# A residual block whose feed-forward part is moved behind all mixing and split into an up and a down stage, with seven half products in place of eight

## The chip, the core and the metric

The kernel runs on one core of a Trainium2 chip. A core has a matrix engine (PE, with a separate queue PEld for loading stationary operands), a vector engine (DVE), a scalar engine (ACT), a general engine (POOL), an on-chip memory SBUF of 128 partitions, and an accumulator memory PSUM that PE writes. All transfers between DRAM and SBUF are issued here by one queue, that of the engine SP, in order; 16 DMA engines carry them out. The engines run side by side and wait for one another through semaphores; each executes its own instructions in the order in which they were built. The metric is the time of one execution in microseconds (us).

## The reference

The input x has 2048 tokens of 1024 features, in float32. One layer is computed:

```
h   = RMSNorm_pre(x)
P   = h @ w_in            (columns for attention, RWKV-7 mixing and gates)
yA  = chunk-band attention;   yB = RWKV-7 time mixing (a recurrence over time)
m   = sigmoid(gA) * (yA @ proj_a) + sigmoid(gB) * (yB @ proj_b)
x   = x + RMSNorm_post(m @ w_out)
x   = x + RMSNorm_post2(relu(RMSNorm_pre2(x) @ w_up)^2 @ w_down)
```

The change concerns the last line, the feed-forward part (FFN). Its `w_up` is 1024 x 4096 and its `w_down` 4096 x 1024. The recurrence carries a state from token to token, so the groups of tokens below are mixed in order.

## The kernel before

**Groups and phases.** The tokens are cut into NG = 4 groups of G = 512. `run` (L1114) goes through the groups: `phase_rwkv`, then `phase_attention`, then for groups 0 and 2 `phase_merge` (the gated merge and `w_out`), whose result `o` is stored to the DRAM tiles `od` (L1137); for groups 1 and 3 it calls `phase_ffn` on the pair (0, 1) or (2, 3), which begins with that group's own merge. So the order is: mix 0, mix 1, FFN of both, mix 2, mix 3, FFN of both. `phase_merge` takes a generator and advances it between its own products; for groups 0 and 2 that is `phase_norm`, which loads and normalises x of the next group.

**Precision by three products.** A float32 operand is split (`split`, L68) into a rounded high part, cast by ACT (L69), and the rest, a subtraction by DVE (L70). `mm3` (L72) makes each product of a 128 x 128 stationary block and a 128 x 512 moving block with three matmuls: high by high, high by low, low by high. All of them have one line, L78.

**The FFN.** `residual` (L962) adds x and the normalised `o` of a tile of 128 tokens (L970 to L973), stores it to `x1`, normalises it again (`norm_tile`, L278) and transposes it on PE into the high and low tiles `hh`/`hl` (or `hbh`/`hbl` for the other group). The hidden units are cut into 32 blocks `fb` of 128. `load` brings a 512 KB block of `w_up` and one of `w_down` to SBUF and splits them (L1028 to L1038). `up` (inside `phase_ffn`) multiplies the block with one group's tokens (24 matmuls into `ps_u`), applies relu on ACT (L1045) and the square on DVE (L1046), and splits the result. `down` accumulates two blocks (6 matmuls into a `ps_dn`) and DVE adds them to the sums `u` and `o` in SBUF (L1064). The first two pairs of blocks run for one group alone, and are loaded again for the other, while the residuals of the second group are still being made. `final` normalises the sums (L1074 to L1082) and stores the output (L1083). While the last pair of the first FFN runs, `phase_norm` of group 2 is advanced.

**What sets the order.** Tiles come from pools with a fixed number of buffers; a tile's new use waits until the readers of the old one are done. Weight blocks are loaded into the tag `raw` with two buffers. The instructions are placed by a scheduler when the program is built, so their order on an engine can differ from that of the source; after that it is fixed.

Of the kernel before, what the change touches and what calls it, by code (L numbers as in the profile page):

```python
# [8 lines left out]
F32 = mybir.dt.float32  # L9
# [40 lines left out]
class Block:  # L50
# [70 lines left out]
    def constants(self, ctx):  # L121
# [128 lines left out]
        self.od = [dp.tile([P, D], F32, name=f"od{t}") for t in range(GT)]  # L250
# [711 lines left out]
    def residual(self, mp, pt, g, t, o, gp, g2, hf):  # L962

        nc = self.nc
        ts = slice(t * P, (t + 1) * P)
        x = mp.tile([P, D], F32, tag="x", name="xr")
        nc.sync.dma_start(x, self.a["x"][g * G + t * P : g * G + (t + 1) * P])
        sq = mp.tile([P, D], F32, tag="xn", name="sqo")
        ssq = mp.tile([P, 1], F32, tag="ssqo", bufs=4, name="ssqo")
        nc.scalar.activation(sq, o, AF.Square, accum_out=ssq)  # L970
        r = self.rstd(mp, ssq, 0.25 / D, RMS_EPS, post=0.5)
        nc.vector.scalar_tensor_tensor(o, o, r, gp, op0=ALU.mult, op1=ALU.mult)
        nc.vector.tensor_tensor(x, x, o, ALU.add)  # L973
        nc.sync.dma_start(self.x1[g][ts], x)
        self.norm_tile(mp, pt, x, g2, *hf, ts)


    def phase_ffn(self, gs, following):

        tc, nc, a = self.tc, self.nc, self.a  # L980
        TH = len(gs)
        GB, NT = 2, TH * GT
        with ExitStack() as ctx:
            e = ctx.enter_context
            hb = e(tc.tile_pool(name="hb", bufs=1, reuse_waits="tile"))
            h = [self.alloc_h()] + [
                (hb.tile([P, KB, G], F32R, tag="hh", name="hbh"), hb.tile([P, KB, G], F32R, tag="hl", name="hbl"))
                for _ in gs[1:]
            ]
            hh, hl = zip(*h)  # L990
# [3 lines left out]
            cp = e(tc.tile_pool(name="ffu", bufs=1, reuse_waits="tile"))  # L994
            o = [cp.tile([P, D], F32, name=f"o{t}") for t in range(GT)]
            gains = []

            def before():
                gains.append(self.gain(op, a["post_mix_g"], "g_post", 2))
                gains.append(self.gain(op, a["pre_ffn_g"], "g_pre2", 2))  # L1000
                if TH > 1:
                    with tc.tile_pool(name="prev", bufs=2, side="right", reuse_waits="tile") as qp:
                        for t in range(GT):
                            q = qp.tile([P, D], F32, tag="o", name="o_prev")
                            nc.sync.dma_start(q, self.od[t])
                            self.residual(op, pt, gs[0], t, q, *gains, h[0])
                            yield

            self.phase_merge(gs[-1], o, before())

            def residuals():
                for t in range(GT):
                    self.residual(op, pt, gs[-1], t, o[t], *gains, h[-1])
                    yield

            res = residuals()
            if TH == 1:
                advance(res)
            cp = e(tc.tile_pool(name="ffc", bufs=1, reuse_waits="tile"))
            u = [cp.tile([P, D], F32, name=f"u{t}") for t in range(NT - GT)] + o  # L1020
            fp = e(tc.tile_pool(name="ff", bufs=2, reuse_waits="tile"))
            pn = e(tc.tile_pool(name="ffpd", bufs=4, space=PSUM, reuse_waits="tile"))
            first = [(fg, (th,)) for th in range(TH) for fg in range(2)]
            for fg, ths in first + [(fg, range(TH)) for fg in range(2, FF // P // GB)]:
                fbs = range(fg * GB, (fg + 1) * GB)
                wu, wd, acts = {}, {}, {}

                def load(fb):  # L1028
                    wu[fb] = self.wsplit(
                        a["w_up"][:, fb * P : (fb + 1) * P].rearrange("(k p) n -> p k n", p=P), "w", KB, P  # L1030
                    )
                    raw = self.wp.tile([P, KB, P], F32, tag="raw", name="wdraw")
                    raw = raw.rearrange("p k n -> p (k n)")
                    nc.sync.dma_start(raw, a["w_down"][fb * P : (fb + 1) * P])
                    dh = fp.tile([P, D], F32R, tag="dh", bufs=3, name="dh")
                    dl = fp.tile([P, D], F32R, tag="dl", bufs=3, name="dl")
                    self.split(dh, dl, raw)
                    wd[fb] = dh, dl  # L1038

                def up(fb, th):  # L1040
                    wh, wl = wu[fb]
                    ps = self.pd.tile([P, 512], F32, tag="d", name="ps_u")
                    self.mm3(ps, [(wh[:, k], wl[:, k], hh[th][:, k], hl[th][:, k]) for k in range(KB)])
                    r = fp.tile([P, 512], F32, tag="r", name="r")
                    nc.scalar.activation(r, ps, AF.Relu)  # L1045
                    nc.vector.tensor_tensor(r, r, r, ALU.mult)  # L1046
                    ah = fp.tile([P, 512], F32R, tag="ah", bufs=5, name="ah")
                    al = fp.tile([P, 512], F32R, tag="al", bufs=5, name="al")
                    self.split(ah, al, r)
                    acts[fb, th] = ah, al  # L1050

                def down(th):
                    for t in range(th * GT, (th + 1) * GT):
                        for n in range(2):
                            ps = pn.tile([P, 512], F32, tag="dn", name="ps_dn")
                            ns, sl = slice(n * 512, (n + 1) * 512), slice((t % GT) * P, (t % GT + 1) * P)
                            self.mm3(ps, [
                                (acts[fb, th][0][:, sl], acts[fb, th][1][:, sl], wd[fb][0][:, ns], wd[fb][1][:, ns])
                                for fb in fbs
                            ])  # L1060
                            if fg == 0:
                                nc.vector.tensor_copy(u[t][:, ns], ps)
                            else:
                                nc.vector.tensor_tensor(u[t][:, ns], u[t][:, ns], ps, ALU.add)  # L1064

                def final(th):
                    for t in range(th * GT, (th + 1) * GT):
                        g, ts = gs[th], slice((t % GT) * P, (t % GT + 1) * P)
                        x = op.tile([P, D], F32, tag=("x", "xn")[t % 2], name="x1r")
                        nc.sync.dma_start(x, self.x1[g][ts])  # L1070
                        ssq = op.tile([P, 2], F32, tag="ssq", bufs=4, name="ssqu")
                        for n in range(2):
                            sq = fp.tile([P, 512], F32, tag="r", name="squ")
                            nc.scalar.activation(  # L1074
                                sq, u[t][:, n * 512 : (n + 1) * 512], AF.Square, accum_out=ssq[:, n : n + 1]
                            )
                        nc.gpsimd.tensor_tensor(ssq[:, 0:1], ssq[:, 0:1], ssq[:, 1:2], ALU.add)
                        r = self.rstd(op, ssq[:, 0:1], 1.0 / D, RMS_EPS)
                        nc.vector.tensor_tensor(u[t], u[t], gt, ALU.mult)  # L1079
                        for n in range(2):  # L1080
                            ns = slice(n * 512, (n + 1) * 512)
                            nc.vector.scalar_tensor_tensor(u[t][:, ns], u[t][:, ns], r, x[:, ns], op0=ALU.mult, op1=ALU.add)  # L1082
                        nc.sync.dma_start(self.out[g * G + ts.start : g * G + ts.stop], u[t])  # L1083

                last = fg == FF // P // GB - 1
                if last:
                    gt = self.gain(op, a["post_ffn_g"], "g_post2", 2)
                if last:
                    for fb in fbs:
                        load(fb)  # L1090
                    for th in ths:
                        for fb in fbs:
                            up(fb, th)
                        if th == 0:
                            norm = iter(()) if following is None else self.phase_norm(following, op, pt)
                            advance(norm, 2)
                        if th == TH - 1:
                            advance(norm)
                        down(th)
                        final(th)  # L1100
# [77 lines left out]
```

## Time and profile before

| | us |
|---|---|
| median of three runs | 3515.34 (3513.74 to 3517.0) |
| profiled execution, its own time | 3517.12 |
| span of that execution, first to last instruction | 3515.4 |
| PE busy | 3381.9 |
| DVE busy | 2160.0 |
| ACT busy | 1362.0 |
| POOL busy | 295.7 |

The profile shows one execution. Busy time of PE counts each matmul from its start to a modelled end; matmuls overlap, so that their number in a stretch says more of PE's rate than their durations do. A row of the grouped view gives source line, engine, operation, the tile written and the tiles read, shape and count, then the busy time and the mean of one in ns, then how long the engine sat idle just before and who ended that. A row of the view by stretches gives for each engine busy time and count, then the granted clock of PE, the share of the DMA engines and what they moved in GB/s.

### The profile page before, as it was taken

The page shows a single profiled execution, that of the slowest core. Times are in us where ns is not written, and L with a number is a line of the kernel's source. Part 1 is how long each engine was busy: PE and PEld are TensorE (multiplying, and loading weights), DVE is VectorE, ACT ScalarE, POOL GpSimd, SP SyncE. Part 2 cuts the span into 40 slices and gives each one's busy share as a digit, 9 for nine tenths or more (in the row PEclk, how much of TensorE's full clock was granted, in tenths as well). Part 3 has the DMA queues.
Part 4 walks back from the last instruction along what each step waited for, and adds up shares of the span by engine and source line. Part 5 has one row for each costly group of instructions (what it writes and reads, how often), then busy time and mean ns, then how long its engine had stood idle before and what let it go on. Part 6 is the DMA issues. An engine that isn't in the chain of part 4 may idle for free. (4 is left out here: it accounts for less than half of the span.)

```text
span 3515.4 us, 49861 instructions
## 1 busy us (share of the span) xinstructions
PE 3381.9 (96%) x19617; PEld 2738.6 (78%) x19617; DVE 2160.0 (61%) x3842; ACT 1362.0 (39%) x2355; POOL 295.7 (8%) x572
## 2 busy tenths in 40 slices
PE   7999999999999999999999999999999899999998
PEld 5777777777777888888877778777777778888887
DVE  5775757757767444444667568577577664444446
ACT  4434644436544111122334366444375532122122
POOL 2210002100011000000121000021000100000001
PEclk9999999999999999999999999999999999999999
DMA  4223453225464111111332253531344641111112
GB/s 145 80 85 124 148 185 101 61 91 177 144 220 156 49 50 52 49 48 48 113 100 62 93 178 126 186 98 56 99 152 127 216 144 48 48 48 49 52 50 78
DMA packets 370851, 363.63 MB, mean 103 GB/s; under 512 B 14572, under 2 KB 293296, under 8 KB 370616
## 3 DMA queue, kind: packets, MB, share of 16 engines
q1 hardware_dynamic: 370616, 360.44, 32.4%
q8 instruction: 154, 2.52, 0.3%
q14 instruction: 81, 0.66, 0.1%
HBM read 293.25 MB, written 70.28 MB: 103 GB/s over the span
## 5 line engine op out<-in xcount | busy, mean ns | idle before, releaser
L70 DVE TENSOR_TENSOR wlo<-wraw,whi 128x1024 fp32r<-128x1024 f32 (+1 forms) x368 | 380.9, 1035 | 416.4 <-ACT whi L69 352.0
L69 ACT CAST whi<-wraw 128x1024 fp32r<-128x1024 f32 (+1 forms) x368 | 331.8, 902 | 752.7 <-PE psd L78 400.5
L78 PE MATMUL psd<-hh,whi 128*128 128x512 f32 x1344 | 544.5, 405 | 11.8 <-ACT whi L69 6.6
L78 PE MATMUL psd<-hl,whi 128*128 128x512 f32 x1344 | 542.2, 403 | 0.0
L78 PE MATMUL psd<-hh,wlo 128*128 128x512 f32 x1344 | 539.0, 401 | 0.6 <-DVE wlo L70 0.5
L78 PE MATMUL ps_dn<-dh,ah 128*128 128x512 f32 x1024 | 400.5, 391 | 9.0 <-ACT ah L69 8.9
L78 PE MATMUL ps_dn<-dl,ah 128*128 128x512 f32 x1024 | 398.6, 389 | 0.0
L78 PE MATMUL ps_dn<-dh,al 128*128 128x512 f32 x1024 | 398.2, 390 | 0.0
L69 ACT CAST dh<-wdraw 128x1024 fp32r<-128x1024 f32 x72 | 75.8, 1052 | 625.7 <-PE ps_dn L78 500.5
L78 PEld LDWEIGHTS psd<-hh,whi 128*128 128x128 f32 x1344 | 257.2, 191 | 65.7 <-ACT whi L69 7.4
L78 PEld LDWEIGHTS psd<-hh,wlo 128*128 128x128 f32 x1344 | 257.3, 191 | 51.1 <-DVE wlo L70 2.0
L78 PEld LDWEIGHTS psd<-hl,whi 128*128 128x128 f32 x1344 | 257.7, 192 | 48.6
L1064 DVE TENSOR_TENSOR o<-o,ps_dn 128x512 f32<-128x512 f32 x240 | 164.1, 688 | 147.2 <-PE ps_dn L78 147.1
L78 PEld LDWEIGHTS ps_dn<-dh,ah 128*128 128x128 f32 x1024 | 192.2, 188 | 53.1 <-ACT ah L69 13.7
L78 PEld LDWEIGHTS ps_dn<-dh,al 128*128 128x128 f32 x1024 | 192.2, 188 | 41.0 <-DVE al L70 1.2
L78 PEld LDWEIGHTS ps_dn<-dl,ah 128*128 128x128 f32 x1024 | 192.4, 188 | 39.3
L1064 DVE TENSOR_TENSOR u<-u,ps_dn 128x512 f32<-128x512 f32 x240 | 161.3, 685 | 81.5 <-PE ps_dn L78 81.3
L78 PE MATMUL ps_u<-hh,wlo 128*128 128x512 f32 x512 | 199.5, 390 | 1.8 <-DVE wlo L70 1.8
L78 PE MATMUL ps_u<-hh,whi 128*128 128x512 f32 x512 | 199.7, 390 | 0.0
L78 PE MATMUL ps_u<-hbh,wlo 128*128 128x512 f32 x512 | 199.4, 389 | 0.0
L78 PE MATMUL ps_u<-hl,whi 128*128 128x512 f32 x512 | 199.2, 389 | 0.0
L78 PE MATMUL ps_u<-hbh,whi 128*128 128x512 f32 x512 | 199.2, 389 | 0.0
(284 smaller groups left out, 6072.5 us busy)
## 6 DMA issues: line engine op xcount, KB each, us to landing
wraw<-in_w_in_dram SPq DMA_DIRECT2D x168, 512.0 KB
wraw<-in_w_up_dram SPq DMA_DIRECT2D x72, 512.0 KB
wdraw<-in_w_down_dram SPq DMA_DIRECT2D x72, 512.0 KB
gd<-gate SPq DMA_DIRECT2D x64, 256.0 KB
th<-gd SPq DMA_DIRECT2D x64, 256.0 KB
wraw<-in_w_out_dram SPq DMA_DIRECT2D x64, 256.0 KB
bias<-skew SPq DMA_DIRECT2D x32, 320.0 KB
x<-in_x_dram SPq DMA_DIRECT2D x16, 512.0 KB
```

Source lines behind the costliest of these rows:

```text
L69: self.nc.scalar.copy(hi, src)
L70: self.nc.vector.tensor_tensor(lo, src, hi.bitcast(F32), ALU.subtract)
L78: mm = nc.tensor.matmul(ps, l, r, start=n == 0, stop=n == last).ins
L1064: nc.vector.tensor_tensor(u[t][:, ns], u[t][:, ns], ps, ALU.add)
```

## The change

`run` mixes all four groups first. Each merge stores its `o` to `od[g]`, and the generator that is advanced beside the merge is now `after`: `phase_norm` of the next group and then `residuals` of the group before. `residuals` is the old `residual` for four tiles, except that it loads `o` from DRAM and writes the transposed result, unsplit, to the DRAM tile `ht[g]`. After the mixing come, for the groups (0, 1) and then (2, 3), `phase_up` and `phase_down`. The residuals of group 3 are advanced within the first `phase_down`.

`phase_up` takes the hidden blocks in pairs (2i, 2i+1) and both groups at once. With the features halved, the pair's weights are four blocks a11, a12 (block 2i, lower and upper features) and a21, a22 (block 2i+1); the tokens are B11, B21 (first group, lower and upper features) and B12, B22 (second group). Instead of eight products of 12 matmuls it makes seven, of sums and differences that DVE and POOL form: `s12` (a21 + a22, and that less a11) and `s34` (a11 - a21, and a12 less the former difference) of the weights, and t1 to t4 of the tokens, made once per `phase_up` by `operands`. Products are added up by DVE (`q`, `w`, and in `hidden`), relu and square follow, and the activation goes to the DRAM tiles `ad` in float32. The first two products of the first eight pairs (`early`) run ahead, beside `operands`; the first one is kept in the tile `z`. `phase_down` loads a block of `w_down` and its activations, splits both, and accumulates as before. In the built program the matmuls into `ps_u` are 2688 in place of 3072, those into `ps_dn` 3072 in both. Its order of SP, DVE and PE was read too; where the prediction speaks of an order in the changed kernel, that is its source.

```diff
@@ class Block
-    def residual(self, mp, pt, g, t, o, gp, g2, hf):
-    def phase_ffn(self, gs, following):
...
+    def residuals(self, g, mp, pt, bufs=2):
...
+        for t in range(GT):
+            o = mp.tile([P, D], F32, tag="oq", bufs=bufs, name="o_prev")
+            nc.sync.dma_start(o, self.od[g][t])
...
+            nc.vector.scalar_tensor_tensor(o, o, r, gp, op0=ALU.mult, op1=ALU.mult)
+            nc.vector.tensor_tensor(x, x, o, ALU.add)
+            nc.sync.dma_start(self.x1[g][ts], x)
...
+            nc.vector.scalar_tensor_tensor(xn, x, r, g2, op0=ALU.mult, op1=ALU.mult)
+            for h in range(2):
...
+                nc.scalar.copy(f, ps)
+                nc.sync.dma_start(self.ht[g][:, h * 4 : h * 4 + 4, ts], f)
+    def after(self, g, sp, pt):
+        if g + 1 < self.NG:
+            yield from self.phase_norm(g + 1, sp, pt)
+        if g > 0:
+            yield from self.residuals(g - 1, sp, pt)
+    def split_here(self, hi, lo):
+        self.nc.scalar.copy(hi, lo.bitcast(F32))
+        self.nc.vector.tensor_tensor(lo, lo.bitcast(F32), hi.bitcast(F32), ALU.subtract)
+    def phase_up(self, gs, z, cb, pn, early):
...
+            up = e(tc.tile_pool(name="up", bufs=1, side="right", reuse_waits="tile"))
+            bh, bl = self.alloc_h()
...
+            def operands():
+                for k in (0, 2):
+                    ks, kt = slice(k, k + 2), slice(KH + k, KH + k + 2)
+                    nc.sync.dma_start(T["t1"][1][:, ks].bitcast(F32), g1[:, ks])
+                    nc.sync.dma_start(T["b22"][1][:, ks].bitcast(F32), g1[:, kt])
+                yield
+                for k in range(KH):
+                    b = up.tile([P, 2, G], F32, tag="s1", name="b1")
+                    for n, (h, l) in enumerate((B11, B21)):
+                        nc.gpsimd.tensor_tensor(b[:, n], h[:, k].bitcast(F32), l[:, k].bitcast(F32), ALU.add)
...
+                    nc.vector.tensor_tensor(t["t1"], b12, b[:, 0], ALU.subtract)
+                    nc.vector.tensor_tensor(t["t3"], b22, b12, ALU.subtract)
+                    nc.vector.tensor_tensor(t["t2"], b22, t["t1"], ALU.subtract)
+                    nc.vector.tensor_tensor(t["t4"], b[:, 1], t["t2"], ALU.subtract)
+                    yield
+                    for n in t:
+                        self.split(T[n][0][:, k], T[n][1][:, k], t[n])
+                    self.split_here(T["b22"][0][:, k], T["b22"][1][:, k])
+                    yield
...
+            def hidden(src, x, fb, th):
+                r = cb.tile([P, G], F32, tag="c", name="r")
+                nc.vector.tensor_tensor(r, src, x, ALU.add)
+                nc.scalar.activation(r, r, AF.Relu)
+                nc.vector.tensor_tensor(r, r, r, ALU.mult)
+                nc.sync.dma_start(self.ad[fb][:, th], r)
+            for i in range(early):
+                wh, wl = self.wsplit(cols(2 * i), "w", KB, P)
+                ps = product((wh[:, lo4], wl[:, lo4]), B11, self.pd, "d")
+                nc.scalar.copy(z[:, i], ps)
+                ps = product((wh[:, hi4], wl[:, hi4]), B21, self.pd, "d")
+                hidden(z[:, i], ps, 2 * i, 0)
+                advance(ops, 1)
+            for i in range(FF // P // 2):
+                raw = []
+                for fb in (2 * i, 2 * i + 1):
+                    raw.append(self.wp.tile([P, KB, P], F32, tag="raw", name="wraw"))
+                    nc.sync.dma_start(raw[-1], cols(fb))
...
+                nc.gpsimd.tensor_tensor(s12[:, 0], a21, a22, ALU.add)
+                nc.vector.tensor_tensor(s12[:, 1], s12[:, 0], a11, ALU.subtract)
...
+                self.split(s12h, s12l, s12)
+                nc.gpsimd.tensor_tensor(s34[:, 0], a11, a21, ALU.subtract)
+                nc.vector.tensor_tensor(s34[:, 1], a12, s12[:, 1], ALU.subtract)
...
+                self.split(s34h, s34l, s34)
...
+                self.split(a22h, a22l, a22)
...
+                ps = product((s12h[:, 1], s12l[:, 1]), T["t2"], pn, "dn")
+                nc.vector.tensor_tensor(q, p1, ps, ALU.add)
+                ps = product((s34h[:, 0], s34l[:, 0]), T["t3"], pn, "dn")
+                nc.vector.tensor_tensor(w, q, ps, ALU.add)
+                ps = product((s12h[:, 0], s12l[:, 0]), T["t1"], pn, "dn")
+                hidden(w, ps, 2 * i + 1, 1)
+                nc.vector.tensor_tensor(q, q, ps, ALU.add)
+                hidden(q, product((s34h[:, 1], s34l[:, 1]), T["b22"], pn, "dn"), 2 * i, 1)
+                hidden(w, product((a22h, a22l), T["t4"], pn, "dn"), 2 * i + 1, 0)
+    def phase_down(self, gs, zp, cb, pn, rest):
...
+            def load(fb):
+                pool, tag = (zp, "z") if fb % 4 == 0 else (ring, "op")
+                t = pool.tile([P, 4, D], F32R, tag=tag, name="fop")
...
+                nc.sync.dma_start(raw, a["w_down"][fb * P : (fb + 1) * P])
...
+                nc.sync.dma_start(ar, self.ad[fb].rearrange("p h t -> p (h t)"))
+                self.split(t[:, 0], t[:, 1], raw)
+                self.split(t[:, 2], t[:, 3], ar)
...
+                    x = op.tile([P, D], F32, tag="x", name="x1r")
+                    nc.sync.dma_start(x, self.x1[g][ts])
@@ run
-                if g % half < half - 1:
...
-                    self.phase_ffn(list(range(g + 1 - half, g + 1)), g + 1 if g + 1 < self.NG else None)
+                    self.phase_merge(g, o, self.after(g, sp, pt))
+                    for t in range(GT):
+                        self.nc.sync.dma_start(self.od[g][t], o[t])
...
+            for half in range(self.NG // 2):
+                gs = (2 * half, 2 * half + 1)
+                z = zp.tile([P, 8, G], F32, tag="z", name="z")
+                self.phase_up(gs, z, cb, pn, 8)
+                self.phase_down(gs, zp, cb, pn, self.NG - 1 if half == 0 else None)
```

More of the change, by code (lines that the diff above doesn't have):

```diff
@@ new lines, in phase_up, with product, cols @@
+            ops = operands()
+            advance(ops, 1)
+            for k in range(0, KB, 2):
+                ks = slice(k, k + 2)
+                self.split_here(bh[:, ks], bl[:, ks])
+            def product(l, r, pool, tag):
+                ps = pool.tile([P, G], F32, tag=tag, name="ps_u")
+                self.mm3(ps, [(l[0][:, k], l[1][:, k], r[0][:, k], r[1][:, k]) for k in range(KH)])
+                return ps
+            def cols(fb):
+                return a["w_up"][:, fb * P : (fb + 1) * P].rearrange("(k p) n -> p k n", p=P)
@@ L995, in phase_ffn @@
[L995 to L1085, printed above, removed]
@@ new lines, in down @@
+            def down(th, ws, first):
+                for t in range(th * GT, (th + 1) * GT):
+                    sl = slice(t * P, (t + 1) * P)
+                    for n in range(2):
+                        ps = pn.tile([P, G], F32, tag="dn", name="ps_dn")
+                        ns = slice(n * 512, (n + 1) * 512)
+                        self.mm3(ps, [(w[:, 2, sl], w[:, 3, sl], w[:, 0, ns], w[:, 1, ns]) for w in ws])
+                        if first:
+                            nc.vector.tensor_copy(u[t][:, ns], ps)
+                        else:
+                            nc.vector.tensor_tensor(u[t][:, ns], u[t][:, ns], ps, ALU.add)
@@ L1122, in run @@
             self.pd = e(tc.tile_pool(name="pd", bufs=2, space=PSUM))
-            half = min(2, self.NG)
             with tc.tile_pool(name="p0", bufs=2, reuse_waits="tile") as sp, \
```

149 lines of the change are left out of this document (98 added, 51 removed).

## The prediction

> **What bounds the kernel now.** I read the page's first part, then a stretch inside the first FFN, then the grouped view of PE.
>
> ```profile
> span 3515.4 us, 49861 instructions
> PE 3381.9 (96%) x19617; PEld 2738.6 (78%) x19617; DVE 2160.0 (61%) x3842; ACT 1362.0 (39%) x2355; POOL 295.7 (8%) x572
> 1300.00:1700.00 400.00, 400.00 (x1765) 331.16 (x1765) 190.68 (x259) 79.06 (x108) 0.00 (x0) 1.00 0.16 48
> L78 PE MATMUL ps_dn<-dh,ah 128*128 128x512 f32 x1024 | 400.5, 391 | 9.0 <-ACT ah L69 8.9
> L78 PE MATMUL ps_u<-hh,wlo 128*128 128x512 f32 x512 | 199.5, 390 | 1.8 <-DVE wlo L70 1.8
> ```
>
> PE is busy for 96% of the span. In the stretch it is busy throughout and runs 1765 matmuls in 400 us: one per 0.2266 us, though one lasts 390 ns, since they overlap. So a matmul taken from the FFN is worth 0.2266 us. The granted clock is 1.00 and DMA moves 48 GB/s. The two rows with idle time show that the FFN's matmuls waited 10.8 us in all. The FFN is bound by PE, and DVE is busy for 190.68 of 400 us beside it; what hides everything else there is this slack.
>
> **The matmuls removed.** 3072 - 2688 = 384 matmuls fewer, 384 x 0.2266 = -87.0 us. The matmuls into `ps_dn` stay. This is the whole gain; all that follows may give it back. The 10.8 us of waits in the old FFN go with its code, and new ones stand in their place: -11.
>
> One rule to weigh: the trace's pitch is 0.2266 us over 1765 matmuls. The Trainium skill, TensorE: Matmul & The Clock Gate, section Back-to-back issue gap, puts a sustained stream of weight loads and matmuls at about 131 ns each for N = 512, and the isolated gap at N / 2.4 GHz + 2.5 ns, 216. By the first the 384 matmuls would be worth 50 us and the sum of the steps would be +8; by the second 83, and -25. The trace disagrees with the first by far and with the second by 5%, and the measurement decides; nothing below hangs on it.
>
> **What DVE, ACT and POOL get to do.**
>
> ```profile
> L70 DVE TENSOR_TENSOR wlo<-wraw,whi 128x1024 fp32r<-128x1024 f32 x240 | 292.9, 1221 | 328.4 <-ACT whi L69 264.3 <-ACT SV L575 46.4 <-PE ps_yt L639 16.8
> L1064 DVE TENSOR_TENSOR u<-u,ps_dn 128x512 f32<-128x512 f32 x240 | 161.3, 685 | 81.5 <-PE ps_dn L78 81.3
> L1046 DVE TENSOR_TENSOR r<-r 128x512 f32<-128x512 f32 x128 | 88.0, 687 | 78.0 <-ACT r L1045 78.0
> L69 ACT CAST whi<-wraw 128x1024 fp32r<-128x1024 f32 x240 | 252.5, 1052 | 596.5 <-PE psd L78 396.9 <-PE ps_u L78 148.8 <-issue 25.4
> L389 POOL TENSOR_TENSOR mN<-mI,n x32: 1044/1495/1910, 68.3 to 2447.4; 128x512 f32<-128x512 f32 x32
> L419 DVE TENSOR_TENSOR BK<-tk,Ei x32: 676/681/1547, 63.8 to 2446.4; 64x512 f32<-64x512 f32 x32
> 102.93 3.00 POOL L389 TENSOR_TENSOR mN<-mI,n 128x512 f32<-128x512 f32 x2
> 103.47 1.55 DVE L419 TENSOR_TENSOR BK<-tk,Ei 64x512 f32<-64x512 f32 x1
> ```
>
> A DVE operation on 128x512 takes 0.69 us, one on 128x1024 1.22; a cast of 1024 on ACT 1.05. POOL adds 128x512 in 1.04 us at best. The last four rows show a collision: the DVE operation at 103.47 ran into POOL's pair and took 1.55 us where 0.68 is usual, so one POOL addition costs DVE up to 0.87.
>
> *Early products.* Each half has 8 pairs x 24 matmuls = 192 x 0.2266 = 43.5 us of PE. DVE has, in the same part: 8 weight splits x 1.22 = 9.8; 8 `hidden` x 2 x 0.69 = 11.0; token operands, 4 x (4 differences + 5 splits) = 36 x 0.69 = 24.8; the first weight sums, 3 x 0.69 + 2 x 1.22 = 4.5. Sum 50.1, which is 6.6 more than PE. POOL's 8 additions collide, at most 8 x 0.87 = 7.0. So DVE bounds this part, by 13.6 us per half. Behind its waiting splits stand the casts' results and the PSUM buffers of the next pair, so PE stops with it. Beside that, `z` waits in the first half until four stores of `od` (2 MB) have landed, and in the second the loads of t1 and b22 stand in SP's queue behind the last store of `final`.
>
> ```profile
> 520.00:532.10 12.10, 11.85 (x53) 9.50 (x52) 5.15 (x7) 6.84 (x11) 2.12 (x7) 1.00 0.88 304
> ```
>
> At these 304 GB/s four such stores take 6.9 us, of which 43.5/8 = 5.4 us are covered by the first pair; the wait for t1 and b22 is spent on three other splits and `hidden`s. Bounds: 5 per half, if DVE's operations follow each other faster than their durations say, and 25, if the waits add fully. I take 14, the sum of work: +28.
>
> *Pairs 0 to 7.* PE: 60 x 0.2266 = 13.6 us a pair. `raw` has two buffers, and both are taken by one pair. In the order of DVE the pair's `s12` difference stands behind the previous pair's first `q`, and a22's split, last reader of the second buffer, near the pair's end. So there is a ring: a22's split frees the buffer, SP issues the next pair's load, it lands, POOL adds a21 + a22, and DVE runs from `s12` to the next a22 split: 10 x 0.69 + 2 x 1.22 = 9.3 us. POOL's 1.04 finds DVE waiting, so it collides with nothing; the subtraction after it costs 0.87 at most. A load:
>
> ```profile
> 1338.40 0.38 SPq L62 DMA_DIRECT2D wraw<-in_w_up_dram  x1
> 1339.40:1342.20 2.80, 2.80 (x14) 2.32 (x13) 2.44 (x5) 0.24 (x1) 0.00 (x0) 1.00 0.69 187
> ```
>
> Issue at 1338.40, 187 GB/s from 1339.40 to 1342.20 (524 KB): 3.8 us. Ring: 9.3 + 1.04 + 0.87 + 3.8 = 15.0 us, 1.4 over PE. Sixteen such pairs in two halves: 22; the first two of each half live on what was loaded ahead, about 2 off: +20. Bounds: 0, if the collision is absent and DVE's operations overlap, and 60, if stores of activations hold up each load by 2.5 us.
>
> *Pairs 8 to 15.* PE: 84 x 0.2266 = 19.0 us. From `s12` to a22's split DVE has 13 x 0.69 + 3 x 1.22 = 12.6; with the same rest the ring takes 18.3. Hidden by 0.7 us: 0, up to 30 if the load takes 2.5 us more.
>
> *ACT* has 2.6 casts of 1024 and three to four relus (0.59 each) a pair, under 6 us: 0; without that cover it would stand in the ring. *Stores and loads of activations*: 128 stores of 256 KB and 64 loads of 512 KB, about 2 MB a pair or a step, 100 to 150 GB/s against 304 shown: 0.
>
> **The down stage.** Per two blocks PE has 96 x 0.2266 = 21.8 us; DVE 16 x 0.69 + 4 x 1.22 = 15.9; ACT 4 x 1.05. Tiles are double-buffered, and group 3's residuals fit into the 6 us left: 0. The step from up to down has three splits ahead of the first sums, two stages, 1.5 each: +3. At the end, `final` has two x1 buffers where it had four: one more load's wait, 0 to 3.8; I take 2, as the sums' own chain runs beside it.
>
> **The residuals and the norm that move.** Group 2's norm was free inside the first FFN and goes to the merge of group 1; residuals 0 and 1 follow the merges of groups 1 and 2, and in DVE's order three of their four tiles stand at the start of the next mixing phase, whose weight loads stand behind their stores in SP's queue.
>
> ```profile
> L972 DVE SCALAR_TENSOR_TENSOR o_prev<-o_prev,rs_p,g_post 128x1024 f32<-128x1024 f32 x8 | 10.3, 1284 | 8.6 <-POOL rs_p L99 8.4
> 1750.00:1850.00 100.00, 95.05 (x448) 75.28 (x446) 73.17 (x117) 40.99 (x69) 28.35 (x51) 0.97 0.32 103
> ```
>
> A tile takes DVE 2 x 1.28 + 1.22 = 3.8 us, three 11.4, and mixing leaves DVE idle for a quarter of the time (73.17 of 100 us busy), PE for a twentieth. Bounds per start: 0, and 11.4 plus one load of 3.8. I take half, 8, for two starts: +16.
>
> **Sum.** -87 - 11 + 28 + 20 + 0 + 3 + 2 + 16 = -29 us against the profiled execution's own 3517.1, which is 1.8 above the median; against the median 3515.3 this is 3486.
>
> **Rivals.** (a) *POOL and DVE exclude each other throughout.* The same row allows it: then all 48 of POOL's additions in the early parts and pairs 0 to 7 cost DVE 1.04 us, 50 in place of 14 + 14 = 28: -29 + 22 = -7, 3508. Against it: half of these find DVE waiting anyway. The Trainium skill, SBUF, section SBUF: two separate sides, states such an exclusive lock for a DVE instruction with two SBUF inputs against a GpSimd one that reads SBUF: the loser blocks for the whole instruction. The trace agrees as far as it shows it (1547 ns against 681); whether it holds for all 48 no row tells.
>
> (b) *The cover holds.* DVE's operations overlap and mixing absorbs the residuals: the early parts cost 5 each, the ring nothing, starts 4 each: -98 + 10 + 5 + 8 = -75, 3440. For it: PE waited only 10.8 us in the old FFN. Against: DVE's surplus of work in the early parts is counted, not guessed.
>
> (c) *The two weight buffers make it slower.*
>
> ```profile
> SPq L62 <- DMA wraw<-in_w_in_dram: 14.3, 6, 7.1
> ```
>
> Where a load shares the queue, waits of up to 7.1 us for one are there. With a load of L the ring takes 11.2 + L and 14.5 + L; the loss over two halves is 16(L - 2.4) + 16(L - 4.5) where positive. It decides from L = 5.1, where the loss reaches 49. At L = 6.0 it is 82 in place of 20: -29 + 62 = +33, 3548. Against: a single load takes 3.8, and only one store of 256 KB stands just ahead.
>
> That the products are not fewer is excluded by their count in the built program.
>
> **Chances.** Forecast (3455 to 3500) 0.50, (a) and its like, down to no change, 0.15, (b) 0.13, (c) 0.22. A measurement here can tell 0.2%, 7 us. Faster: 0.50 + 0.13 and two thirds of (a), 0.73; within 0.2%: 0.05; slower 0.22. The range reaches from (b)'s 3440 to 3550, past (c)'s middle; the forecast's own is 3455 to 3500.
>
> **What will show it.** The count of matmuls into `ps_u` at 2688. PE's idle time before `ps_u`, by what ended it: DVE's t splits in the early parts (28 us), `s12l` or `s34l` in pairs 0 to 7 (20 us), none in pairs 8 to 15. DVE's idle time before `s12`, ended by POOL, is the ring; 16 pairs of 15.0 us would prove it. `ps_dn` at 21.8 us per two blocks. Wrong would be a pair of 8 to 15 over 19.0 us, loads over 5 us, `ps_dn` waiting for its splits, or mixing of groups 2 and 3 longer by more than 30 us.

## The result, and the profile after

The changed kernel takes 3569.8 us (median of 4 runs, 3562.9 to 3571.7) beside 3514.5 for the kernel before: ratio 1.0151, 95% interval 1.0138 to 1.0163. It is 1.5% slower; forecast was 3486 with a range to 3550. The profiled execution has a span of 3569.8 us, 54.4 more than that of before. The first part of its page:

```profile
span 3569.8 us, 50854 instructions
PE 3357.2 (94%) x19233; PEld 2692.1 (75%) x19233; DVE 2430.9 (68%) x4162; ACT 1428.3 (40%) x2419; POOL 396.4 (11%) x652
```

The 384 matmuls are gone, and with them 25 us of PE's busy time, not 87; DVE and POOL have gained 271 and 101 us. Where the time went is read by stage. I cut both traces at the first and last matmul of each stage (merge ends with the last `ps_o`, up with the last `ps_u`, down with the last `ps_dn`). In the window view a row has the stretch and its length, then the busy time and count of PE, PEld, DVE, ACT and POOL, the granted clock, the share of the DMA engines and GB/s. After: mixing of groups 0 to 3, up and down of the first half, up of the second half, the last down with the tail:

```profile
0.00:526.20 526.20, 484.79 (x3190) 382.02 (x3191) 336.89 (x742) 241.40 (x462) 61.61 (x130) 0.97 0.40 124
526.20:1044.50 518.30, 497.39 (x3399) 398.99 (x3398) 349.80 (x694) 255.81 (x455) 56.46 (x111) 0.99 0.41 132
1044.50:1580.70 536.20, 505.94 (x3430) 404.73 (x3429) 360.43 (x704) 265.73 (x475) 62.24 (x128) 0.98 0.43 136
1580.70:2120.00 539.30, 507.63 (x3429) 407.57 (x3430) 368.29 (x705) 269.48 (x480) 65.53 (x137) 0.97 0.42 135
2120.00:2478.40 358.40, 328.24 (x1345) 259.02 (x1344) 236.51 (x303) 116.30 (x166) 54.80 (x38) 0.96 0.40 128
2478.40:2842.80 364.40, 358.05 (x1575) 294.74 (x1574) 271.44 (x355) 91.19 (x124) 18.97 (x39) 0.99 0.41 134
2842.80:3204.40 361.60, 326.34 (x1341) 257.12 (x1340) 248.91 (x319) 117.17 (x168) 62.42 (x46) 0.96 0.39 125
3204.40:3569.80 365.40, 348.86 (x1537) 287.93 (x1535) 258.63 (x344) 71.28 (x94) 14.34 (x24) 0.99 0.34 107
```

The same view of the kernel before, groups 0 to 3 and the two FFNs between and behind them:

```profile
0.00:520.80 520.80, 481.82 (x3190) 379.60 (x3191) 336.85 (x742) 241.56 (x462) 61.58 (x130) 0.98 0.40 125
520.80:1041.70 520.90, 497.17 (x3397) 399.13 (x3397) 356.48 (x699) 256.85 (x457) 58.06 (x118) 0.99 0.41 133
1041.70:1754.40 712.70, 706.58 (x3138) 582.60 (x3137) 379.57 (x503) 181.45 (x272) 30.18 (x47) 1.00 0.24 73
1754.40:2275.90 521.50, 498.09 (x3398) 400.21 (x3397) 354.10 (x702) 253.82 (x453) 56.97 (x116) 0.99 0.38 120
2275.90:2795.20 519.30, 495.21 (x3397) 398.26 (x3397) 356.21 (x699) 256.52 (x457) 58.01 (x118) 0.99 0.39 126
2795.20:3515.40 720.20, 703.05 (x3105) 578.75 (x3103) 376.77 (x500) 171.77 (x257) 30.95 (x44) 1.00 0.22 68
```

The four groups take 2120.0 against 2082.5 us: +37.5, of which groups 2 and 3 have 14.7 and 20.0. The FFN itself (up, down, up, down to the last matmul at 3554.1) takes 1434.1 against 1421.6: +12.5 with 384 matmuls fewer. The tail behind the last matmul takes 15.7 against 11.3. Sum 54.4.

An up stage of 1344 matmuls at 0.2266 us would take 304.6 us; it takes 358.4 and 361.6, and the granted clock there is 0.96. Cut once more, at the first product of pair 0 and the first of pair 8:

| | PE alone | first half | second half | loss, both | predicted |
|---|---|---|---|---|---|
| early products | 43.5 | 61.7 | 64.1 | 39 | 28 |
| pairs 0 to 7 | 108.8 | 123.3 | 122.4 | 28 | 20 |
| pairs 8 to 15 | 152.3 | 173.6 | 175.2 | 44 | 0 |

The waits behind it, in the grouped view (busy us, mean ns, then idle time before the group and what ended it):

```profile
L1100 DVE TENSOR_TENSOR s<-s,wraw 128x512 f32<-128x512 f32 x32 | 56.4, 1761 | 136.1 <-POOL s L1099 136.1
L78 PE MATMUL ps_u<-t4h,a22h 128*128 128x512 f32 x128 | 55.9, 437 | 23.6 <-DVE q L1119 23.6
L78 PE MATMUL ps_dn<-fop 128*128 128x512 f32 x3072 | 703.6, 391 | 7.2 <-DVE q L1124 5.0
```

DVE waits 136.1 us for POOL's `s12`, over 4 us a pair: the ring. At `s12l`, where I looked for it, PE stops for only 8.1 us, nearly all in pairs 0 to 7; in pairs 8 to 15 it stops at the product of a22, which waits for DVE's first `q`. PE works ahead until the four PSUM buffers of the five products are full; `q`, which would empty one, stands behind DVE's wait for POOL.

One pair of 8 to 15 in the timeline (start, duration, engine; in brackets the idle time before and what ended it; PE left out):

```profile
2338.63 1.29 POOL L1099 TENSOR_TENSOR s<-wraw 128x512 f32<-128x512 f32 x1 [19.32 <-DMA wraw<-in_w_up_dram]
2339.88 1.29 POOL L1103 TENSOR_TENSOR s<-wraw 128x512 f32<-128x512 f32 x1
2339.96 1.77 DVE L1100 TENSOR_TENSOR s<-s,wraw 128x512 f32<-128x512 f32 x1 [4.51 <-POOL s L1099]
2341.76 0.69 DVE L1104 TENSOR_TENSOR s<-wraw,s 128x512 f32<-128x512 f32 x1
...
2342.51 0.38 SPq L1091 DMA_DIRECT2D wraw<-in_w_up_dram  x1
...
2346.93 1.05 ACT L69 CAST whi<-wraw 128x1024 fp32r<-128x1024 f32 x1 [10.81 <-DMA wraw<-in_w_up_dram]
2347.88 1.05 ACT L69 CAST s12h<-s 128x1024 fp32r<-128x1024 f32 x1
2348.01 1.22 DVE L70 TENSOR_TENSOR wlo<-wraw,whi 128x1024 fp32r<-128x1024 f32 x1 [3.57 <-ACT whi L69]
...
2350.34 1.22 DVE L70 TENSOR_TENSOR s12l<-s,s12h 128x1024 fp32r<-128x1024 f32 x1
...
2355.02 0.68 DVE L70 TENSOR_TENSOR a22l<-wraw,a22h 128x512 fp32r<-128x512 f32 x1
...
2355.73 0.38 SPq L1091 DMA_DIRECT2D wraw<-in_w_up_dram  x1
...
2360.33 1.29 POOL L1099 TENSOR_TENSOR s<-wraw 128x512 f32<-128x512 f32 x1 [19.16 <-DMA wraw<-in_w_up_dram]
```

The period is 21.7 us, and it contains two loads. L1104 is the last reader of the pair's first block; SP then loads the next pair's first block (2342.51), which lands at 2346.9. ACT casts it and DVE splits it (`wlo`) **before** they split the present pair's `s12`: so the program orders them. Only after that come `s12l`, `s34l` and `a22l`, which frees the second block, and its load takes 2355.73 to 2360.33, 4.60 us. From 2311 to 2465 us DVE waits 34.7 us for POOL's `s12` (seven times) and 21.6 us for ACT's `whi` (six times), both behind a load, and never for PE: a slower PE does not lengthen this ring.

The residual rows at the start of mixing, by the first `ps_A` matmul after each merge: 54.5 us from the end of merge 1, 55.0 from merge 2, where group 1 in the same kernel, without residuals, needs 38.3.

### The profile page after: what moved, and what is told of

The parts are those of the page before. It is cut to its first block, busy times and chain, and to the rows that moved or that the text cites. A ratio compares the mean times of both kernels' runs of the same rounds, so it can differ in the third digit from the quotient of the medians.

```text
span 3569.8 us, 50854 instructions
## 1 busy us (share of the span) xinstructions
PE 3357.2 (94%) x19233; PEld 2692.1 (75%) x19233; DVE 2430.9 (68%) x4162; ACT 1428.3 (40%) x2419; POOL 396.4 (11%) x652
## 5 line engine op out<-in xcount | busy, mean ns | idle before, releaser
L78 PE MATMUL ps_dn<-fop 128*128 128x512 f32 x3072 | 703.6, 391 | 7.2 <-DVE q L1124 5.0
L78 PEld LDWEIGHTS ps_dn<-fop 128*128 128x128 f32 x3072 | 578.3, 189 | 130.4 <-DVE q L1124 5.4
L1162 DVE TENSOR_TENSOR u<-u,ps_dn 128x512 f32<-128x512 f32 x480 | 323.6, 685 | 181.3 <-PE ps_dn L78 180.8
L1100 DVE TENSOR_TENSOR s<-s,wraw 128x512 f32<-128x512 f32 x32 | 56.4, 1761 | 136.1 <-POOL s L1099 136.1
L78 PE MATMUL ps_p<-yh,whi 128*128 128x512 f32 x256 | 107.8, 421 | 23.8 <-DVE th L930 23.1
L78 PE MATMUL ps_u<-hh,whi 128*128 128x512 f32 x256 | 103.6, 405 | 17.0 <-DVE r L1072 10.1
L78 PE MATMUL ps_u<-hh,wlo 128*128 128x512 f32 x256 | 102.6, 402 | 6.9 <-DVE wlo L70 6.8
L956 PE MATMUL ps_o<-wlo,mh 128*128 128x512 f32 x256 | 102.2, 399 | 5.2 <-DVE wlo L70 5.2
L829 ACT ACTIVATE sc<-sc,mn 128x640 f32<-128x640 f32 (+4 forms) x128 | 97.8, 764 | 21.1 <-DVE mn L824 20.4
L78 PE MATMUL ps_p<-yl,whi 128*128 128x512 f32 x256 | 105.5, 412 | 0.0
L78 PE MATMUL ps_p<-yh,wlo 128*128 128x512 f32 x256 | 105.5, 412 | 0.0
```

The source lines that it names most:

```text
L78: mm = nc.tensor.matmul(ps, l, r, start=n == 0, stop=n == last).ins
L829: nc.scalar.activation(sc[:, 0:n], sc[:, 0:n], AF.Exp, scale=-1.0, bias=mn, accum_out=sm)
L956: nc.tensor.matmul(ps[t], l[:, k, ts], r[:, 0], start=k == 0 and j == 0, stop=k == KB - 1 and j == 2)
L1100: nc.vector.tensor_tensor(s12[:, 1], s12[:, 0], a11, ALU.subtract)
```

## The experiments

Each was timed beside the kernel before on the same chip (3518.5 to 3519.0 us there); ratios are to it. Stretches and pairs are read from each run's trace as above; line numbers shift by a few lines with the edits.

**The order alone.** `issue_after` puts what follows behind a named instruction in its engine's order; `behind` holds the cast and the subtraction of a22.

```
-                    self.split(wh, wl, raw[0])
+                    with tc.issue_after(behind[0]), tc.issue_after(behind[1]):
+                        self.split(wh, wl, raw[0])
...
-                self.split(a22h, a22l, a22)
+                behind = self.split(a22h, a22l, a22)
```

> Edit: the split of the next pair's first weight block is put behind the a22 split of the present pair in the orders of ACT and DVE; nothing else. Theory (ring of two buffers, with two loads one behind the other in pairs 8 to 15, 22.2 us a pair): one of the two loads leaves the ring, which falls to 4.6 + 1.3 + 11.0 = 17.0 us, under PE's 19.0; pairs 8 to 15 fall by 3.2 us each, 16 x 3.2 = -51, to 3519 us (3510 to 3530); pairs 0 to 7 stay at 15.4. Rival (POOL and DVE exclude each other and that lengthens the pairs): no change, 3565 to 3575. Rival (the four PSUM buffers of the five products): no change either.

3520.8 us, ratio 1.0007 (0.9998 to 1.0016). The up stages:

```profile
2114.30:2452.40 338.10, 321.52 (x1346) 256.48 (x1345) 240.13 (x307) 120.10 (x171) 54.82 (x38) 0.97 0.43 140
2809.70:3148.80 339.10, 318.44 (x1341) 253.81 (x1340) 249.69 (x319) 118.25 (x168) 63.81 (x46) 0.97 0.42 133
```

They are 20.3 and 22.5 us shorter. The ring of pairs 8 to 15 settles at 19.4 to 19.6 us, with no wait of PE, and that of pairs 0 to 7 stays at 15.3. Pairs 8 to 15 take 156.1 us in each half, where 173.6 and 175.2 were measured. So the second load in the ring, put there by the order, cost 37 of the 44 us there, and some 6 in the pairs just before. The other 7 remain: PE itself takes 19.5 us a pair, not 19.0, which the padding runs explain. Both rivals fall as the cause of what the ring costs in pairs 8 to 15.

**More buffers.**

```
-                for fb in (2 * i, 2 * i + 1):
-                    raw.append(self.wp.tile([P, KB, P], F32, tag="raw", name="wraw"))
-                    nc.sync.dma_start(raw[-1], cols(fb))
+                if i < early:
+                    raw.append(self.wp.tile([P, KB, P], F32, tag="wh", name="wraw"))
+                else:
+                    if i == early:
+                        zr = zp.tile([P, 4, KB, P], F32, tag="z", name="zraw")
+                    raw.append(zr[:, i % 4])
+                raw.append(self.wp.tile([P, KB, P], F32, tag="raw", name="wraw"))
+                for n, x in enumerate(raw):
+                    nc.sync.dma_start(x, cols(2 * i + n))
```

> Edit: two more buffers for weight blocks in pairs 0 to 7 (those of the unused split tiles) and four in pairs 8 to 15 (the space of z, then free); the order of the work as it is. Theory (ring): no load stands in the ring, so all pairs run at PE's pace, 13.6 and 19.0 us: -14 x 1.8 - 16 x 3.2 = -76, 3494 us (3485 to 3510). Rival (collision): the collisions stay, so no change, 3565 to 3575. Rival (PSUM buffers): no change.

3511.6 us, ratio 0.9977 (0.9967 to 0.9988). The ring is gone, but 18 us are missing: behind the first of each kind (17.8 to 18.0 and 20.6 to 20.8) the pairs run without a wait of PE at 14.06 and 19.49 us, not at 13.6 and 19.0. In the trace the matmuls on weight blocks follow each other at 0.227 us from start to start (their pitch), as everywhere in the FFN before, and those on the sums and a22 at 0.234. 1920 x 0.0072 = 14 us of the 18. The padding run below takes that up.

**POOL's additions on DVE.**

```
-                nc.gpsimd.tensor_tensor(s12[:, 0], a21, a22, ALU.add)
+                nc.vector.tensor_tensor(s12[:, 0], a21, a22, ALU.add)
```

and the same at `s34[:, 0]` and `b1`.

> Edit: POOL's 80 additions run on DVE. Theory (ring): the ring loses POOL's 1.29 and the collision's 1.08 and gains two additions of 0.6 to 0.69 on DVE, -1.1 us a pair, 32 x 1.1 = -35, 3535 us (3525 to 3550); loads still stand in the ring. Rival (collision is the cause of all of the loss in the up stage): pairs at PE's pace, 3490 to 3500.

3515.9 us, ratio 0.9995 (0.9985 to 1.0005), 19 better than expected. In the first up stage, where the subtraction took 1763 ns beside POOL:

```profile
L1099 DVE TENSOR_TENSOR s<-wraw 128x512 f32<-128x512 f32 x15 | 10.4, 693 | 48.0 <-DMA wraw<-in_w_up_dram 48.0
L1100 DVE TENSOR_TENSOR s<-s,wraw 128x512 f32<-128x512 f32 x15 | 10.3, 686 | 0.0
```

The collision is 1.08 us a pair, and DVE still waits for loads. Pairs 0 to 7 fall from 15.3 to between 14.0 and 14.3 in the first half, most pairs of 8 to 15 from 22.2 to about 21.3: some 1 us a pair, as the ring has it. The two up stages are 50 us shorter: 17 in pairs 0 to 7, 25 in pairs 8 to 15, of which the first three or four of each half now run at PE's 19.5, and 8 in the early parts (3.4 and 4.7), which I had set at zero: there the collisions of `b1` are gone. In total this is as fast as e1_order, so the totals do not tell the collision from the second load. Pairs 8 to 15 do: they come down to PE's pace where the collisions stay and the second load leaves the ring, and stay above it, at about 21.3, where the collisions leave and the second load stays. Collision is a part of the ring's length, not a limit by itself.

**The staging alone.** The up stage is a plain loop over 32 blocks of `w_up` and two halves of tokens, 24 matmuls into one PSUM tile each, relu on ACT, square on DVE, store.

> Edit: the new staging alone: the up stage forms eight half products as whole products (3072 matmuls in place of 2688), without sums, early products and token operands; mixing, stores, down stage and residuals as in the changed kernel. Theory (staging costs by itself the longer mixing, +38, the step from up to down, up to +10, and the tail, +4): 3515 + 45 = 3560 us (3550 to 3572). Rival (all of the loss is in the seven products): as before, 3515 (3508 to 3522).

3549.7 us, ratio 1.0095 (1.0080 to 1.0110). The staging costs 31 us by itself: its mixing ends at 2112.9, 30 later than before, its tail 4.7 longer. Its FFN, 1418.5 us, is 3 shorter than before. So of the changed kernel's 55 us some 31 to 35 are staging and some 20 to 24 the seven products (timed apart: the kernel before took 3514.5 us beside the one and 3519.0 beside the other), which gave 87 and took over 100.

**Padding.** Against e2_buffers, one tile of 96 bytes a partition at the head of the right side of SBUF:

```
+            e(tc.tile_pool(name="pad", bufs=1, side="right")).tile([P, 24], F32, name="pad")
```

The built program places the split sums, the split a22 and the operands `yh`, `yl` of the merge 32 bytes past a multiple of 64; the weight blocks, the token operands and the down operands stand on multiples of 128.

> Edit against e2_buffers: 96 bytes of padding at the head of the right side of SBUF, so that the sums, their splits and the mixing operands there start at a multiple of 128 bytes; in e2_buffers they start 32 past a multiple of 64. No instruction changes. Theory (a weight operand off the 64-byte grid makes a matmul slower: the products of the sums run at 0.2342 us a matmul in e2_buffers, those of the weights at 0.2272): 1920 matmuls x 0.0072 = -14, and some -2 from the 768 into ps_p, to 3496 us against e2_buffers' 3512. Rival (the pitch has another cause, such as the products' length or PSUM buffers): no change, 3508 to 3516.

3493.8 us, ratio 0.9927 (0.9912 to 0.9942), -18. PE is busy throughout in both of these stretches of 80 us in pairs 0 to 7, first e2_buffers:

```profile
2200.00:2280.00 80.00, 80.00 (x343) 64.28 (x343) 59.18 (x80) 24.34 (x33) 18.51 (x11) 1.00 0.39 122
```

and with the padding:

```profile
2195.00:2275.00 80.00, 80.00 (x355) 66.24 (x354) 62.26 (x82) 26.34 (x35) 18.84 (x12) 1.00 0.39 125
```

355 matmuls in place of 343 at the same granted clock of 1.00. The median pitch of every one of the fifteen kinds of sum matmul goes from 232 to 235 ns to 227.

**The same padding elsewhere.**

> Edit against the changed kernel: only the 96 bytes of padding of e5_align. Theory (its pairs are bound by the ring, not by PE): the faster matmuls of the sums find PE waiting, -2 for the mixing and up to -5 for the steps where PE is the limit, 3563 to 3570 us, though the same padding gave -18 on e2_buffers. Rival (the pairs are bound by PE's pitch in part): -14 to -18, 3552 to 3556.

3566.1 us, ratio 1.0136 (1.0121 to 1.0152) beside the changed kernel's 1.0151: some 5 us, with intervals that overlap. The sums' matmuls have a pitch of 0.227 here too, but the ring hides a PE that is 3% faster on them.

> Edit against the kernel before: only the 96 bytes of padding. Theory (the padding helps matmuls whose weights lie on the right side, and before that is ps_p alone, 768 matmuls at 0.234 us): -2 to -6, 3513 to 3517 us beside 3518. Rival (the padding helps by something else too): more than -8.

3518.7 us, ratio 0.9999 (0.9990 to 1.0009): no change that can be measured, so the theory's 2 to 6 us are not shown. Of the 768 matmuls into `ps_p` only the 384 of the merge have a moving operand that the padding shifts; without those that follow a wait or stand in a slow spell, their mean pitch falls from 0.234 to 0.229, under 2 us in all. The other 384 stay at about 0.234.

**The early parts.** Against e2_buffers, `nc.scalar.activation(r, r, AF.Square)` in place of DVE's `r * r`.

> Edit against e2_buffers: the square of each activation is taken on ACT in place of DVE. Theory (the early products are bound by DVE's sum of work, as predicted): 8 x 0.69 = 5.5 us less on DVE in each early part, -11, to 3501 us; the rest of the up stage is at PE's pace and does not change. Rival (the early parts wait for transfers: z for the stores of the mixed rows, t1 and b22 for their loads): no change, 3508 to 3516.

3508.2 us, ratio 0.9963 (0.9948 to 0.9977), -3.5: neither of the two. Taking 5.5 us from DVE gives some 2 a half. In e2_buffers' first early part DVE is busy for 47.4 of 61.9 us, so the sum of its work is not what bounds it; PE waits 4.0 us for `z` (ACT's copy waits for a store of `od`) and 3.6 for DVE's `r`. In the second, DVE works almost the whole time (57.2 of 62.2 us), for a reason that I had not counted (window of that part):

```profile
L1186 DVE SCALAR_TENSOR_TENSOR u<-u,rs_r,x1r 128x512 f32<-128x512 f32 x8 | 6.7, 874 | 0.0
L1183 DVE TENSOR_TENSOR u<-u,g_post 128x1024 f32<-128x1024 f32 x4 | 5.9, 1489 | 0.0
```

These 12.6 us are the first half's `final`, which runs into the next up stage. How the rest divides was not separated.

**The residual rows.** Against e2_buffers:

```
-        if g > 0:
-            yield from self.residuals(g - 1, sp, pt)
+        for done in {1: (0,), 3: (1, 2)}.get(g, ()):
+            yield from self.residuals(done, sp, pt)
```

> Edit against e2_buffers: residuals(1) stands beside merge 3, ahead of residuals(2), and no longer beside merge 2. Theory (residual rows that spill over the end of a merge hold PE's transposes, DVE and SP's queue at the start of the next mixing phase, 16 us a phase): from the end of merge 2 to the first chunk of rwkv(3) 55 us become 38 to 40, and mixing of group 3 is 520 to 524 long up to the start of merge 3; the four tiles come back at the end, 0 to 32 us by what covers them there. Rival (the longer mixing comes from other places in DRAM or SBUF, or from the norm): 55 us stay.

3516.9 us, ratio 0.9994 (0.9984 to 1.0004). From merge 2 to the first `ps_A`, in e2_buffers:

```profile
1580.70:1635.50 54.80, 45.35 (x206) 35.02 (x204) 33.45 (x39) 29.49 (x51) 17.25 (x38) 0.94 0.63 202
```

and without residual rows there, with the stretch behind merge 3 where the four rows now stand:

```profile
1577.10:1615.30 38.20, 37.83 (x174) 30.22 (x173) 22.43 (x30) 18.94 (x31) 11.16 (x21) 1.00 0.51 165
2098.90:2136.70 37.80, 7.90 (x33) 6.30 (x33) 13.93 (x12) 14.13 (x24) 8.65 (x17) 0.56 0.90 288
```

16.6 us, as expected, only 3.5 of them the 32 transposes. Behind merge 3 nothing covers the rows; they cost 37.8, of which the next up stage gives 12 back, nearly all in its early part, where the operands are ready.

**A version faster than both.** Against e2_buffers:

```
+            e(tc.tile_pool(name="pad", bufs=1, side="right")).tile([P, 24], F32, name="pad")
-                        nc.gpsimd.tensor_tensor(b[:, n], h[:, k].bitcast(F32), l[:, k].bitcast(F32), ALU.add)
+                        nc.vector.tensor_tensor(b[:, n], h[:, k].bitcast(F32), l[:, k].bitcast(F32), ALU.add)
-                nc.vector.tensor_tensor(r, r, r, ALU.mult)
+                nc.scalar.activation(r, r, AF.Square)
-                    x = op.tile([P, D], F32, tag="x", name="x1r")
+                    x = op.tile([P, D], F32, tag=("x", "xn")[t % 2], name="x1r")
```

> Edit against e2_buffers: padding of e5_align, squares on ACT as in e6_square, the 16 additions for b1 on DVE, and four buffers for the last rows of x1 as before. If the theories behind e5 and e6 hold: 3512 - 16 - 11 - 4 (last rows) - 3 (collisions in the early parts) = 3478 us, 1.1% under the kernel before; with the rivals 3505 to 3512.

3479.0 us, ratio 0.9884 (0.9868 to 0.9901): 1.2% under the kernel before. Its up stages:

```profile
2114.70:2436.40 321.70, 311.05 (x1346) 254.98 (x1345) 200.98 (x255) 159.84 (x234) 52.62 (x32) 0.98 0.46 147
2791.40:3112.20 320.80, 309.26 (x1335) 252.74 (x1334) 206.81 (x263) 156.12 (x231) 53.51 (x37) 0.98 0.43 136
```

They are 16 to 17 us over PE's 304.6, where the changed kernel is 54 and 57 over. Its mixing is still some 32 us longer than before. That the time meets the expected 3478 is in part luck: squares on ACT were priced at 11 us after e6's theory and gave 3.5 alone, while squares, `b1` and the buffers of x1 together make the two early parts 5.7 and 7.0 shorter than in e5_align. What each gives beside the other was not separated.

**Rows closer together.** Against e8_all, `tag="sq" if bufs == 2 else "xn"` for the squared row.

> Edit against e8_all: the square of each residual row in a merge gets a tile of its own, so that the next row's square does not wait for a buffer of the row before. Theory (the spill of residual rows into rwkv(2) and rwkv(3) is a chain of latencies, some 7 to 8 us a row, lengthened by the two shared buffers): the rows stand closer, 4 to 8 us less at the start of each of the two phases and 2 to 4 in merge 3, -10 to -20, to 3459 to 3469 us. Rival (the spill is set by the work of DVE and the transposes, whose sum does not change): 3475 to 3483.

3483.6 us, ratio 0.9905 (0.9885 to 0.9924): no gain. The idea of the two shared buffers fell; from merge 1 to the first `ps_A` it is 54.9 us, 54.4 in e8_all. What sets the spill's length is open.

## Why the prediction was wrong

By the traces, in the prediction's order of terms (-87 - 11 + 28 + 20 + 0 + 3 + 2 + 16): -87 for the matmuls, -29 for the old FFN's waits and extra work, +39 early, +28 and +44 for the pairs, +18 for the down stages and their step, +4 for the tail, +35 for mixing of groups 2 and 3, and +3 for groups 0 and 1, which had no term: +55. The largest single miss is the 44 at 0; without it the kernel would still be 40 us over the forecast, by the residuals, the down stage and the early parts above all.

- **The matmuls removed, -87.** Right as a count (2688 into `ps_u`). The pitch of 0.2266 holds on operands that stand as those of before do; the sums stand elsewhere in SBUF and cost 0.234, 14 us less gain, most of which only shows once the ring is gone. The -11 for the old FFN's waits was too little: before is 29 us over 6144 matmuls at 0.2266, transposes among them.
- **Pairs 8 to 15, "Hidden by 0.7 us: 0, up to 30": the step that failed.** Measured 44, of which 37 are the ring and 7 PE's pace on the sums. I counted `wlo` among DVE's work between `s12` and a22's split, but not what it waits for: it belongs to the next pair, and its block is loaded only when the present pair's `s34` is done. The ring had two loads of some 4.6 us in it and took 22.2 us, not 18.3. e1_order shows it: with the order alone changed, 19.5.
- **Pairs 0 to 7, 15.0 us.** Measured 15.3: the ring is there, but its length is near by luck. The load was 4.6 in place of 3.8, the collision 1.08 in place of 0.87 and POOL's addition 1.29 in place of 1.04, while DVE's operations start 0.60 us apart in place of 0.69 (1.14 in place of 1.22), which makes 8.3 of the 9.3. PE feels the ring late in each half: pairs 1 to 3 run at its own 14.06. The loss was 28 in place of 20, some 7 of it PE's pace on the sums.
- **Early products, +28.** Measured 39. The reason given, that DVE's sum of work bounds this part, is not borne out in the first half, where DVE is busy for 47.5 of 61.7 us and e6_square gains little: it is a chain of waits of PE for DVE, ACT and a store. In the second half DVE is near its limit, but with `final` on it, which was missing. How the 39 divide is open.
- **The down stage, 0, and the step to it, +3.** The second half is 1.6 us over 348.1. The first is 16.3 over: 3.5 are transposes of group 3's residuals, 7 waits at the step, 4 slow matmuls behind them (last section). There DVE idles 8.8 us at L1009, the split of the **next** half's operands, which its order puts ahead of the last activations; again work of the next stage that waits for a load.
- **Residuals, +16.** Measured 35 in groups 2 and 3, 16.6 a start in e7_residual: a little over the upper bound of the step (15.2), not its half. PE stands in it too: its transposes wait in its own order for DVE's `xn`.
- **The tail, +2.** 4.4.
- **The rivals.** (a) The exclusion held in all 32 pairs (subtractions of 1.73 to 1.77 us); the Trainium skill, SBUF — State Buffer, section SBUF: two separate sides, puts it as an exclusive lock, and the trace agrees. It did not decide pairs 8 to 15: e1_order keeps the collisions and runs them at PE's pace. In the rest of the up stage it counts, as e3_no_pool shows with 25 us in the early parts and pairs 0 to 7, POOL's own time in the ring included. (b) fell. (c) named the right place, the two weight buffers, and was right on the side; its price came from a second load, not from a long one. (Its own formula reaches 49 at L = 5.0, not 5.1.)

Among the signs, a pair of 8 to 15 over 19.0 us and mixing longer by more than 30 were named as what would make it wrong; both came.

## What to carry to other kernels

When a load is double-buffered, walk the ring from the release of a buffer round to its next release in the **built order of each engine**, and ask of every instruction on the way what it waits for; one that belongs to the next turn brings the next turn's load into this one. Such work can be held back with an order edge that costs nothing (49 us here) or given buffers from tiles that are dead in that stage. Before a gain in matmuls is priced at a neighbour's pitch, look where the new operands will stand.

## What the runs showed of the hardware

**Placement in SBUF.** Stationary operands that start 32 bytes past a multiple of 64 gave matmuls of 512 columns a pitch of 0.234 us in place of 0.227, at a granted clock of 1.00 (e2_buffers and e5_align). For a moving operand there is only e11_before_pad: 0.234 and 0.229. Of the padding's two effects, 64-byte and 128-byte multiples, the runs do not say which is the one, and the placement is not the only way to 0.234: the other matmuls into `ps_p` have it on multiples of 128.

**A pause of PE costs twice.** After the wait of 2.21 us in the pair above:

```profile
2343.79 0.52 PE L78 MATMUL ps_u<-t4h,a22h 128*128 128x512 f32 x1 [2.21 <-DVE q L1119]
2344.11 0.63 PE L78 MATMUL ps_u<-t4l,a22h 128*128 128x512 f32 x1
2344.53 0.63 PE L78 MATMUL ps_u<-t4h,a22l 128*128 128x512 f32 x1
...
2347.51 0.40 PE L78 MATMUL ps_u<-t4h,a22h 128*128 128x512 f32 x1
```

For 3.7 us the matmuls come 0.43 us apart, then 0.23 again; the granted clock is 0.54 over these 3.7 us and 1.00 on either side. I counted this in the records of ten traces (before, after, e1 to e8), over all waits of PE in front of a matmul of 512 columns, by the time from the start before the wait to the start behind it. A spell is at least two of the next eight matmuls 0.40 to 0.47 us apart. Of waits of 3.5 us and more 67 of 68 brought one, from 2 to 3.5 us 70 of 119, from 1 to 2 us 40 of 307. The trace of before has 121 matmuls of 512 columns that last 0.6 us or more, that of after 294. The Trainium skill, TensorE: Matmul & The Clock Gate, section What's actually happening, has the clock halved after an idle window of about 3.4 us; the trace agrees above that, and shows more than half of the waits from 2 us on doing it too. It also makes single executions differ: in group 0, where before and after issue the same instructions, a pause of 3.05 us in the profile of after brought a slow spell and one of 1.93 at the same place in that of before did not. By the end of the spell after is 3.6 us behind, most of the 5 us by which group 0 is longer; in those of e1 to e10 merge 0 ends at 519 to 522, as before's 520.8.
